# One-hot rows of a gate matrix: one packed bf16 comparison per four tokens, widened by GpSimd and ScalarE

## The chip, the cores and the metric

The kernel runs on one core of a Trainium2 chip. The metric is the device time of one execution in microseconds (us). An execution is profiled once more for the trace; the trace's span runs from the first to the last instruction.

The engines are named as in the profile: PE is TensorE's matrix products (PEld its weight loads), DVE is VectorE, ACT is ScalarE, POOL is GpSimd, SP is SyncE, which issues most of the transfers (DMA). POOL issues the indirect ones.

## What is computed

The reference is one decoder layer over 1024 tokens of width 1024: modulated norm, a mix of retention and stick-breaking attention, and then a feed-forward part of 16384 single-neuron experts. Only that last part is touched here:

```python
def peer(h, w_query, sub_keys, expert_down, expert_up):
    qry = (ht @ w_query).reshape(T, PEER_HEADS, 2, PEER_HALF)
    sub_scores = jnp.einsum('thpc,hpkc->thpk', qry, sub_keys).astype(jnp.float32)
    top_s, top_i = lax.top_k(sub_scores, K)
    ...
    best_s, best_c = lax.top_k(cand_s.reshape(T, PEER_HEADS, K * K), K)
    expert_id = jnp.take_along_axis(cand_id.reshape(T, PEER_HEADS, K * K), best_c, axis=-1)
    gate = jax.nn.softmax(best_s, axis=-1)
    ...
        a = jnp.einsum('pd,ped->pe', xb, u).astype(jnp.float32)
        act = jax.nn.gelu(a, approximate=False) * gb
        return jnp.einsum('pe,ped->pd', act.astype(xb.dtype), v)
```

Each token has 8 heads with 16 chosen experts each, so 128 slots. An expert's number is 128 i1 + i2, where i1 and i2 come from two halves of 128 sub-keys.

## The kernel before

The 1024 tokens are eight tiles of 128. Tiles 0 to 3 are "gathered": for each of their 128 slots the rows of the two expert tables are fetched by an indirect transfer (L767, issued by GpSimd), and VectorE multiplies them with the tokens (L778) or sums them up (L788). That is 1024 gathers in all, through four buffers named g. Tiles 4 to 7 (512 tokens) are "dense": PE computes all 16384 experts for them, in 128 blocks of 128 (`stage1`, L812, and `stage2`, L917), and a gate matrix, zero for the experts that a token has not chosen, multiplies the activations in between (L907).

The instructions are ordered in each engine's queue by a planner that simulates a timeline (`schedule_with_timeline_sim`). The gathers come last in the program and run wherever the rest leaves room; 16 of them, from row 480 on, are held until piece 4 of the gate matrix (`HOLD`, `HOLD_C`).

The gate matrix is built ahead of the dense blocks, at L843 to L876, in 16 pieces of 32 tokens (`CT`), each of eight quads of four tokens. With the 128 slots on partitions, `rt` holds i1, i2 and the gate for each token. For a quad:

- `oa` (128 slots x 4 tokens x 128) is one where i1 equals the column number: a comparison on VectorE (L859). GpSimd multiplies it by the gate (L860).
- `ob` is the same for i2. For three of four quads VectorE compares (L864); for the fourth ScalarE computes max(0, 1 - |i - i2|) in eight instructions (L868, L869).
- PE multiplies them, token by token (L871), which gives 128 x 128 gates of a token, and ScalarE copies the sums out (two copies, at L872 to L874) to `st`, which SP stores (L876).

Between the pieces lie the routing of tiles 5, 6 and 7 (`late`, through `topk`, which ends in `to_slots`) and the first products of early expert blocks (`stage1_ahead`). `stage1` splits the block's weights in two parts for PE: a copy on ScalarE and a subtraction (L810), which `stage1_ahead` gives to GpSimd for n below 8 and for odd n, and otherwise to VectorE. `NSE` is 6 and `NS` is 8; 28 blocks (`NP`) are computed ahead. `oa` and `ob` come from a pool of eleven buffers, `p2`, as do the outputs of some early blocks. `copy` (L70) is ScalarE's activation Copy, so all its instructions stand on L71.

Of the kernel before, what the change touches and what calls it, by code (L numbers as in the profile page):

```python
# [10 lines left out]
F32 = mybir.dt.float32  # L11
F32R = mybir.dt.float32r
BF16 = mybir.dt.bfloat16
I32 = mybir.dt.int32
U32 = mybir.dt.uint32
AF = mybir.ActivationFunctionType
OP = mybir.AluOpType
# [7 lines left out]
SEGS = [(0, 1), (1, 3), (4, 4)]  # L25
NG = 4                      # token tiles whose experts are gathered; the rest see every expert
TD = (NT - NG) * 128
GB = 4                      # expert blocks that share one accumulation
CT = 32                     # tokens of one piece of the gate matrix
NB = 128  # L30
LC = 1, 5, 9                # pieces of the gate matrix ahead of which the next tile is routed
# order of the retention's halves and the stick-breaking projections
RET = "h0 K h1 t0 Q h2 t1 V h3 t2 | t3"
HOLD, HOLD_C = 480, 4      # gathers from row HOLD on wait for piece HOLD_C of the gate matrix
LT0, LATE = 3, (4,)         # gathered tiles from LT0 on are routed ahead of the dense groups from LATE on
# early blocks: PM of a group, NS of them kept on chip, NSE ahead of the gate matrix and NSL behind it
PM, NS, NSE, NSL = 2, 8, 6, 6
NP = 28                     # expert blocks whose first product runs while the gate matrix is built
BIG = 1e15
# [15 lines left out]
def tile_kernel(ctx, tc, A, out):  # L55
# [14 lines left out]
    def copy(out_, in_, scale=1.0):  # L70
        ACT.activation(out_, in_, AF.Copy, scale=scale)  # L71
# [10 lines left out]

    # ------------------------------------------------------------ constants
    ident = cst.tile([128, 128], F32, name="ident")
# [14 lines left out]
    POOL.memset(epsc, EPS)  # L99
    iota128 = cst.tile([128, 128], F32, name="iota128")  # L100
    POOL.iota(iota128, pattern=[[1, 128]], base=0, channel_multiplier=0, allow_small_or_imprecise_dtypes=True)
    iota16 = cst.tile([128, 16], BF16, name="iota16")
# [23 lines left out]

    # ------------------------------------------------------------ modulation and rotary tables
    sc2 = cst.tile([128, 8, 32], F32, name="sc2")
    aw = A["ada_w"].rearrange("(k p) n -> k p n", p=128)

    def mod_pass(c0, nj, W, V):
        # 512 nj columns of silu(c) @ ada_w + ada_b from c0 on, and where they go
        acc = pstile("acc", 4)
        m = 32 * nj
        for kt in range(KT):
            for hf in range(nj // 2):
                w = W(KT * hf + kt)
                SP.dma_start(w, aw[kt, :, c0 + D * hf:c0 + D * hf + D])
                for j2 in range(2):
                    j = 2 * hf + j2  # L140
                    PE.matmul(acc[32 * j:32 * j + 32], sc2[:, kt, :], w[:, 512 * j2:512 * j2 + 512],
                              start=kt == 0, stop=kt == KT - 1, skip_group_check=True)
        brow, modrow = V(), V()
        ab = A["ada_b"]
        for j in range(nj):
            SP.dma_start(brow[32 * j:32 * j + 32], bass.AP(tensor=ab.tensor, offset=ab.offset + c0 + 512 * j,
                                                          ap=[[0, 32], [1, 512]]))
        DVE.tensor_add(modrow[:m], acc[:m], brow[:m])
        tp = pstile("tp", 2)
        for q in range(4):  # L150
            PE.transpose(tp[:, 128 * q:128 * q + m], modrow[:m, 128 * q:128 * q + 128], ident[:m, :m])
        mc = modcol[:, c0 // 128:c0 // 128 + 4 * nj].rearrange("a (j q) -> a j q", q=4)
        DVE.tensor_copy(mc, tp.rearrange("a (q j r) -> a j q r", j=4, r=32)[:, 0:nj, :, 0])
        for j in range(nj):
            v = ("shift1", "scale1", "gate1", "shift2", "scale2", "gate2")[c0 // D + j // 2]
            if v in rows_d:
                SP.dma_start(rows_d[v][:, 512 * (j % 2):512 * (j % 2) + 512], modrow[32 * j:32 * j + 1])
            if v == "scale1" and j % 2:
                DVE.scalar_tensor_tensor(g1s, modcol[:, 8:16], 1.0, n1g, op0=OP.add, op1=OP.mult)
            if v == "scale2" and j % 2:  # L160
                DVE.scalar_tensor_tensor(g2s, modcol[:, 32:40], 1.0, n2g, op0=OP.add, op1=OP.mult)

    with tc.tile_pool(name="ini", bufs=1) as ini:
# [3 lines left out]
        DVE.tensor_copy(sc2, sc[:, :, None].to_broadcast([128, 8, 32]))  # L167
        # sin and cos of position * frequency, reduced exactly in three pieces
        posi = ini.tile([128, NT], I32, name="posi")
# [51 lines left out]

    # ------------------------------------------------------------ gather pools (live through the end)
    gp = ctx.enter_context(tc.tile_pool(name="gp", bufs=1))
# [6 lines left out]
    def seg_gen(phase, t0, nt, hooks):  # L230
        wp, tp_, up, vp, kp = phase
        n = nt * 128
        whole = nt == 1             # one tile alone: float32 products, no split of the weights
        tiles = range(t0, t0 + nt)
# [13 lines left out]
        def stream(src, c0, lhs, evac, transposed):  # L248
            # 512 columns of src from c0 against the operand [128, KT, n]
            acc = [pstile("acc", 4) for _ in range(4 if transposed else nt)]  # L250
# [78 lines left out]

        # ---- norm1 and transposed h  # L330
        xn = []
# [8 lines left out]

        # ---- retention operands
        def rot(acc, o, t):
# [45 lines left out]

        # ---- stick-breaking operands
        def head_norm(acc, o):  # L390
# [28 lines left out]

        # ---- retention  # L420
        def ret_head(i):
# [76 lines left out]

        # ---- stick-breaking attention
        def sb_weights(i, pr):  # L500
# [82 lines left out]

        # ---- output projection, residual
        x1 = []
# [36 lines left out]

        # ---- queries, scores, the 16 best sub-keys of each half
        own = [i for i, t in enumerate(tiles) if t not in sc_d]
# [55 lines left out]
    def topk(kp, v, ix, t, h0, nh):  # L680
# [12 lines left out]
        for h in range(nh):  # L693
# [5 lines left out]
            DVE.max_index(px[:, h, 8:16], bs[:, h, 8:16], c2)  # L699
        # position in the candidate list -> (a, b)  # L700
        pq, qf = K("pq", (2, nh, 16), U32, "w1"), K("qf", (2, nh, 16), F32, "w2")
# [29 lines left out]
        if t < NG:  # L731
            ids = gp.tile([128, nh * 16], I32, name=f"ids_{t}_{h0}")
            DVE.scalar_tensor_tensor(ids, flat(ii[:, 0]), 128.0, flat(ii[:, 1]), op0=OP.mult, op1=OP.add)
        # softmax gates
        e, s = K("ge", (nh, 16)), K("gs", (nh,))
# [14 lines left out]
    def to_slots(t, ii, gt):  # L750
        # routing of this tile with (head, slot) on partitions
        tp = pstile("acc", 4)
        for k, src in enumerate((flat(ii[:, 0]), flat(ii[:, 1]), flat(gt))):
            PE.transpose(tp[:, 128 * k:128 * k + 128], src, ident)
        rt = gp.tile([128, 3, 128], F32, name=f"rt_{t}")
        copy(rt, tp[:, 0:384].rearrange("p (a b) -> p a b", b=128))
        route[t] = rt

# [39 lines left out]
    def dense(Hhi, Hlo, dp, kpg, late):  # L798
# [29 lines left out]
        def stage1_ahead(n):  # L828
            y = stage1(list(pre)[n], POOL if n < NS else (DVE, POOL)[n % 2])
            if n < NS:  # L830
# [11 lines left out]

        # gate matrix, 32 tokens at a time, while the first blocks' products run  # L843
        iota4 = iota128[:, None, :].to_broadcast([128, 4, 128])
        for c in range(TD // CT):
            for k in range(1, 4):
                if c == LC[k - 1]:
                    late[k - 1]()
            rt = route[NG + c * CT // 128]
            st = [U8([128, NB // 2, CT], F32) for _ in range(2)]  # L850
            for q in range(CT // 4):
# [3 lines left out]

                def wide(v):
                    return rt[:, v, t4:t4 + 4, None].to_broadcast([128, 4, 128])

                DVE.tensor_tensor(oa, iota4, wide(0), op=OP.is_equal)  # L859
                r = POOL.tensor_tensor(oa, oa, wide(2), op=OP.mult)  # L860
                if c == HOLD_C:
                    hold = r.ins
                if q % 4:
                    DVE.tensor_tensor(ob, iota4, wide(1), op=OP.is_equal)  # L864
                else:
                    # the same one-hot rows as max(0, 1 - |i - i2|)
                    for k in range(4):
                        ACT.activation(ob[:, k], iota128, AF.Abs, bias=rt[:, 1, t4 + k:t4 + k + 1], scale=-1.0)  # L868
                        ACT.activation(ob[:, k], ob[:, k], AF.Relu, scale=-1.0, bias=1.0)  # L869
                for k in range(4):  # L870
# [17 lines left out]
        for g0 in range(0, NB, GB):  # L888
# [54 lines left out]
            if g0 + GB == NB:  # L943
                # the residual and what is summed up so far, ahead of the last products
                fin = dp2.tile([128, 2, D], F32, name="fin", tag="gm", bufs=2)
# [32 lines left out]

    # the gathers run wherever what is above leaves room
    for t in range(NG):  # L980
# [54 lines left out]
```

## Time and profile before

| | us |
|---|---|
| median of 3 runs | 3257.86 |
| lowest and highest | 3248.1, 3262.58 |
| profiled execution, span | 3254.1 |
| profiled execution, its own device time | not shown by the page |

Where the span goes, by the windows of the trace:

| stretch, us | what it is |
|---|---|
| 0 to 1400 | attention and routing of the first tiles, with gathers among them |
| 1400 to 1527 | routing of tile 4 |
| 1527 to 1886 | gate matrix, early blocks, routing of tiles 5 to 7 |
| 1886 to 3244 | dense blocks, with the rest of the gathers among them |
| 3244 to 3254 | the last sums and stores |

A row of a group of instructions reads: line, engine, operation, output and inputs by the program's names, shapes, count, then busy us and mean ns of one, then the idle time of the engine just before them and what ended most of it. A row of a window gives its length and then, for PE, PEld, DVE, ACT and POOL in turn, the busy time and the number of instructions; then the granted clock of TensorE as a share of full speed, the transfers' share, and GB/s.

### The profile page before, as it was taken

To read this page: it belongs to the slowest core of one execution; us is meant where nothing else is said; L and a number is where in the kernel's file an instruction comes from. 1 tells how busy PE (TensorE), PEld (TensorE's weight loads), DVE (VectorE), ACT (ScalarE), POOL (GpSimd) and SP (SyncE) were. 2 spreads that over 40 slices of the span, in tenths; PEclk is the share of its full clock that TensorE was granted. 3 is DMA by queue.
4 is the path that set the end of the run, shared out by engine and by line. 5 is a ranking of instruction groups with operands and counts; after the bars stand their busy time and mean duration, and the time that the engine had idled before them with its cause. 6 is when DMAs were issued, how large, how long until landed. Compare 5 with 4: busy or idle time off the path is not lost.

```text
span 3254.1 us, 38714 instructions
## 1 busy us (share of the span) xinstructions
PE 2721.3 (84%) x12308; PEld 2102.5 (65%) x12308; DVE 2706.5 (83%) x4997; ACT 1065.1 (33%) x1995; POOL 1956.1 (60%) x1554
## 2 busy tenths in 40 slices
PE   6967867787867678796787799878999999999998
PEld 2454644486654345575666677667787888887786
DVE  2269788799988898799999978999787878777888
ACT  1132223344312344333554532323222322222221
POOL 0026765676677566743577756555666666666664
PEclk9978886898977778897898899998999999999999
DMA  8687876997888666841366789878999999999897
GB/s 317 239 300 271 303 266 218 319 340 258 278 277 281 224 214 226 308 148 65 117 228 211 274 314 329 288 260 297 319 330 328 323 340 339 338 332 319 319 323 273
DMA packets 337644, 899.20 MB, mean 276 GB/s; under 512 B 38296, under 2 KB 105880, under 8 KB 333344
## 3 DMA queue, kind: packets, MB, share of 16 engines
q0 software_dynamic: 147456, 536.94, 47.3%
q1 hardware_dynamic: 189984, 359.80, 32.1%
q8 instruction: 97, 1.59, 0.2%
q14 instruction: 107, 0.88, 0.1%
HBM read 846.24 MB, written 50.35 MB: 276 GB/s over the span
## 4 chain that ended last, share of the span: by engine, by line
DVE 28%; DMA 22%; issue 19%; PE 14%; POOL 14%; ACT 1%; SPq 1%; POOLq 0%; DVEq 0%; ACTq 0%
POOL g L767 9%; DMA g<-in_up_dram,ids 9%; DMA g<-in_down_dram,ids 5%; DVE g L778 5%; DVE gy L788 4%; PE acc L263 2%; DVE p L859 2%; POOL u L810 2%; DMA gm<-gd 2%; DMA rawu<-in_up_dram 1%; POOL wlo L271 1%; DVE p L864 1%; PE acc L871 1%; PE tp L819 1%; PE tp L820 1%
## 5 line engine op out<-in xcount | busy, mean ns | idle before, releaser
L767 POOL DMA_INDIRECT g<-in_up_dram,ids x512 | 583.4, 1139 | 416.3 <-DVE gy L788 295.2
L767 POOL DMA_INDIRECT g<-in_down_dram,ids x512 | 541.6, 1058 | 460.8 <-DVE g L778 280.6
L788 DVE SCALAR_TENSOR_TENSOR gy<-g,a,gy 128x1024 f32<-128x1024 f32 x508 | 651.2, 1282 | 141.2 <-DMA g<-in_up_dram,ids 137.6
L778 DVE SCALAR_TENSOR_TENSOR g<-g,gy 128x1024 f32<-128x1024 f32 x512 | 617.5, 1213 | 133.5 <-DMA g<-in_down_dram,ids 131.3
L928 PE MATMUL acc<-u,p 128*128 128x512 f32 x1024 | 404.6, 400 | 43.5 <-DVE yacc L941 23.9
L819 PE MATMUL tp<-Thi,dhi 128*128 128x512 f32 x1024 | 408.9, 399 | 22.9 <-ACT dhi L71 18.4
L821 PE MATMUL tp<-Thi,dlo 128*128 128x512 f32 x1024 | 405.4, 396 | 3.7 <-POOL dlo L810 3.6
L820 PE MATMUL tp<-Tlo,dhi 128*128 128x512 f32 x1024 | 406.1, 397 | 0.0
L929 PE MATMUL acc<-u,p 128*128 128x512 f32 x1024 | 404.1, 396 | 1.0 <-POOL u L810 1.0
L930 PE MATMUL acc<-u,p 128*128 128x512 f32 x1024 | 386.6, 396 | 15.9 <-DVE p L910 15.9
L810 POOL TENSOR_TENSOR u<-rawu,u 128x1024 fp32r<-128x1024 f32 x128 | 309.0, 2422 | 30.2 <-ACT u L71 28.3
L271 POOL TENSOR_TENSOR wlo<-wraw,whi 128x512 fp32r<-128x512 f32 x182 | 236.6, 1306 | 101.3 <-ACT whi L71 69.1
L928 PEld LDWEIGHTS acc<-u,p 128*128 128x128 f32 x1024 | 195.8, 191 | 99.5 <-DVE yacc L941 32.4
L819 PEld LDWEIGHTS tp<-Thi,dhi 128*128 128x128 f32 x1024 | 196.8, 192 | 65.0 <-ACT dhi L71 19.4
L930 PEld LDWEIGHTS acc<-u,p 128*128 128x128 f32 x1024 | 195.4, 191 | 60.4 <-DVE p L910 19.3
L71 ACT ACTIVATE whi<-wraw 128x512 fp32r<-128x512 f32 x208 | 130.3, 630 | 308.0 <-PE acc L281 100.2
L280 PE MATMUL acc<-wlo,Thi 128*128 128x512 f32 x504 | 214.1, 425 | 18.0 <-POOL wlo L271 17.6
L71 ACT ACTIVATE dhi<-rawd 128x1024 fp32r<-128x1024 f32 x128 | 135.4, 1058 | 284.2 <-PE tp L820 267.2
L71 ACT ACTIVATE u<-rawu 128x1024 fp32r<-128x1024 f32 x128 | 133.2, 1056 | 285.8 <-DMA rawu<-in_up_dram 184.9
L821 PEld LDWEIGHTS tp<-Thi,dlo 128*128 128x128 f32 x1024 | 196.2, 192 | 46.0 <-POOL dlo L810 5.3
L929 PEld LDWEIGHTS acc<-u,p 128*128 128x128 f32 x1024 | 196.0, 191 | 41.2 <-POOL u L810 1.4
L820 PEld LDWEIGHTS tp<-Tlo,dhi 128*128 128x128 f32 x1024 | 196.6, 192 | 39.9
(273 smaller groups left out, 5150.0 us busy)
## 6 DMA issues: line engine op xcount, KB each, us to landing
rawd<-in_downT_dram SPq DMA_DIRECT2D x128, 512.0 KB
rawu<-in_up_dram SPq DMA_DIRECT2D x128, 512.0 KB
gd<-u SPq DMA_DIRECT2D x32, 1024.0 KB
gm<-gd SPq DMA_DIRECT2D x512, 64.0 KB
wraw<-in_w_in_dram SPq DMA_DIRECT2D x112, 256.0 KB
u<-in_ada_w_dram SPq DMA_DIRECT2D x46, 512.0 KB
wraw<-in_wq_dram SPq DMA_DIRECT2D x64, 256.0 KB
u<-in_w_in_dram SPq DMA_DIRECT2D x28, 512.0 KB
```

Of the source, the lines that this page charges most:

```text
L71: ACT.activation(out_, in_, AF.Copy, scale=scale)
L271: (POOL if kt else DVE).tensor_sub(lo, raw, hi.bitcast(F32))
L767: POOL.indirect_dma_start(out=g, out_offset=None, in_=A[src], in_offset=bass.IndirectOffsetOnAxis(ap=groups[j // m][0][:, j % m:j % m + 1] ...
L778: DVE.scalar_tensor_tensor(g, g, 1.0, hp, op0=OP.mult, op1=OP.mult, accum_out=a[:, j:j + 1])
L788: DVE.scalar_tensor_tensor(y, g, a[:, j:j + 1], y, op0=OP.mult, op1=OP.add)
L810: eng.tensor_sub(lo, raw, hi.bitcast(F32))
L819: PE.matmul(a, dhi[:, sl], Hhi[:, kt], start=kt == 0, stop=False)
L820: PE.matmul(a, dhi[:, sl], Hlo[:, kt], start=False, stop=False)
L821: PE.matmul(a, dlo[:, sl], Hhi[:, kt], start=False, stop=kt == KT - 1)
L928: PE.matmul(y, phi[:, sl], uhi[:, ds_], start=st and b == 0, stop=False)
L929: PE.matmul(y, phi[:, sl], ulo[:, ds_], start=False, stop=False)
L930: PE.matmul(y, plo[:, sl], uhi[:, ds_], start=False, stop=sp and b == GB - 1)
```

## The change

Both comparisons of a quad become one VectorE instruction on packed bf16: tile, i1 and i2, column number and token are its axes, `[128, 2, 128, 4]`, with the four tokens innermost. The column numbers are stored four times over in bf16, and the routing of a tile is kept as bf16 numbers (`rb`) and f32 gates (`rg`), by two copies for one. GpSimd's product reads the first half of the result with the axes exchanged, so with a step of four bf16 elements, and writes `oa` in f32. A ScalarE copy does the same for the second half and writes `ob`. The eight ScalarE instructions of every fourth quad are gone. The result `oc` takes a third buffer of `p2` for each quad. The subtraction of the early blocks goes to GpSimd for n below `NSE` and otherwise to VectorE. The rest of the diff is comments.

```diff
-    iota128 = cst.tile([128, 128], F32, name="iota128")
-    POOL.iota(iota128, pattern=[[1, 128]], base=0, channel_multiplier=0, allow_small_or_imprecise_dtypes=True)
+    iota128 = cst.tile([128, 128, 4], BF16, name="iota128")
+    POOL.iota(iota128, pattern=[[1, 128], [0, 4]], base=0, channel_multiplier=0, allow_small_or_imprecise_dtypes=True)
...
     def to_slots(t, ii, gt):
...
-        rt = gp.tile([128, 3, 128], F32, name=f"rt_{t}")
-        copy(rt, tp[:, 0:384].rearrange("p (a b) -> p a b", b=128))
-        route[t] = rt
+        rb = gp.tile([128, 2, 128], BF16, name=f"rb_{t}")
+        copy(rb, tp[:, 0:256].rearrange("p (a b) -> p a b", b=128))
+        rg = gp.tile([128, 128], F32, name=f"rg_{t}")
+        copy(rg, tp[:, 256:384])
+        route[t] = rb, rg
...
-            y = stage1(list(pre)[n], POOL if n < NS else (DVE, POOL)[n % 2])
+            y = stage1(list(pre)[n], POOL if n < NSE else DVE)
...
-        iota4 = iota128[:, None, :].to_broadcast([128, 4, 128])
+        iota8 = iota128[:, None, :, :].to_broadcast([128, 2, 128, 4])
...
-            rt = route[NG + c * CT // 128]
+            rb, rg = route[NG + c * CT // 128]
...
-                def wide(v):
-                    return rt[:, v, t4:t4 + 4, None].to_broadcast([128, 4, 128])
-
-                DVE.tensor_tensor(oa, iota4, wide(0), op=OP.is_equal)
-                r = POOL.tensor_tensor(oa, oa, wide(2), op=OP.mult)
+                oc = P2([128, 2, 128, 4], BF16)
+                DVE.tensor_tensor(oc, iota8, rb[:, :, None, t4:t4 + 4].to_broadcast([128, 2, 128, 4]), op=OP.is_equal)
+                r = POOL.tensor_tensor(oa, oc[:, 0].rearrange("p i t -> p t i"),
+                                       rg[:, t4:t4 + 4, None].to_broadcast([128, 4, 128]), op=OP.mult)
...
-                if q % 4:
-                    DVE.tensor_tensor(ob, iota4, wide(1), op=OP.is_equal)
-                else:
...
-                    for k in range(4):
-                        ACT.activation(ob[:, k], iota128, AF.Abs, bias=rt[:, 1, t4 + k:t4 + k + 1], scale=-1.0)
-                        ACT.activation(ob[:, k], ob[:, k], AF.Relu, scale=-1.0, bias=1.0)
+                copy(ob, oc[:, 1].rearrange("p i t -> p t i"))
```

## Rows read from the trace of the kernel before

**Rows 1.** The page's totals by engine: busy us, share, instructions.

```profile
PE 2721.3 (84%) x12308; PEld 2102.5 (65%) x12308; DVE 2706.5 (83%) x4997; ACT 1065.1 (33%) x1995; POOL 1956.1 (60%) x1554
```

**Rows 2.** Windows: busy us of each engine, granted clock, DMA share, GB/s.

```profile
1527.00:1886.00 359.00, 277.33 (x1549) 240.89 (x1548) 349.31 (x485) 195.46 (x575) 260.28 (x183) 0.88 0.57 203
1886.00:3244.00 1358.00, 1292.25 (x5561) 1052.09 (x5559) 1137.14 (x1629) 378.22 (x490) 848.39 (x632) 0.98 0.90 317
...
2000.00:2300.00 300.00, 258.73 (x1055) 205.04 (x1055) 279.38 (x608) 85.61 (x109) 177.89 (x130) 0.93 0.85 289
2300.00:2600.00 300.00, 293.42 (x1280) 240.49 (x1279) 247.49 (x245) 82.79 (x107) 192.56 (x143) 0.99 0.92 328
2600.00:2900.00 300.00, 298.74 (x1316) 246.45 (x1315) 240.74 (x369) 87.46 (x112) 198.10 (x152) 1.00 0.95 337
```

**Rows 3.** Groups by line, VectorE, 1527 to 1886 us.

```profile
L859 DVE TENSOR_TENSOR p<-iota,rt 128x512 f32<-128x512 f32 x128 | 146.6, 1154 | 0.0
L864 DVE TENSOR_TENSOR p<-iota,rt 128x512 f32<-128x512 f32 x96 | 88.6, 923 | 7.2 <-PE acc L871 7.2
...
L810 DVE TENSOR_TENSOR dlo<-rawd,dhi 128x1024 fp32r<-128x1024 f32 x9 | 13.8, 1529 | 0.0
...
L726 DVE TENSOR_TENSOR oh<-oh,iota 128x2048 bf16<-128x2048 bf16 x6 | 9.4, 1574 | 2.0 <-ACT oh L71 2.0
```

**Rows 4.** Groups by line, GpSimd, 1527 to 1886 us.

```profile
L860 POOL TENSOR_TENSOR p<-p,rt 128x512 f32<-128x512 f32 x128 | 165.6, 1304 | 79.4 <-DVE p L859 78.4 <-PE acc L871 0.5
...
L810 POOL TENSOR_TENSOR dlo<-rawd,dhi 128x1024 fp32r<-128x1024 f32 x12 | 32.4, 2703 | 0.8 <-ACT dhi L71 0.7
```

**Rows 5.** Timeline, VectorE and GpSimd, 1706.5 to 1712: start us, us.

```profile
1708.10 2.95 DVE L711 TENSOR_TENSOR qf<-qf,m 128x128 f32<-128x128 f32 x1
1710.97 0.28 DVE L710 TENSOR_TENSOR ab<-ab,m 128x128 f32<-128x128 f32 x1
...
1707.86 3.03 POOL L860 TENSOR_TENSOR p<-p,rt 128x512 f32<-128x512 f32 x3
```

**Rows 6.** Single lines, whole run: duration ns min/median/max, first and last start.

```profile
L859 DVE TENSOR_TENSOR p<-iota,rt x128: 637/680/4717, 1527.3 to 1878.2; 128x512 f32<-128x512 f32 x128
...
L726 DVE TENSOR_TENSOR oh<-oh,iota x34: 398/426/3356, 197.1 to 2252.2; 128x512 bf16<-128x512 bf16 x24, 128x2048 bf16<-128x2048 bf16 x10
...
L860 POOL TENSOR_TENSOR p<-p,rt x128: 1028/1058/8106, 1528.0 to 1880.2; 128x512 f32<-128x512 f32 x128
...
L810 POOL TENSOR_TENSOR dlo<-rawd,dhi x18: 2342/2406/3356, 1507.3 to 1897.9; 128x1024 fp32r<-128x1024 f32 x18
```

**Rows 7.** Groups by line, ScalarE, whole run.

```profile
L71 ACT ACTIVATE whi<-wraw 128x512 fp32r<-128x512 f32 x208 | 130.3, 630 | 308.0 <-PE acc L281 100.2 <-DMA wraw<-in_w_in_dram 92.7 <-DMA wraw<-in_wq_dram 47.4
...
L868 ACT ACTIVATE p<-iota,rt 128x128 f32<-128x128 f32 x128 | 40.9, 412 | 0.0
...
L869 ACT ACTIVATE p<-p 128x128 f32<-128x128 f32 x128 | 31.5, 323 | 0.0
```

**Rows 8.** Waits, 1527 to 1886: us in total, times, longest.

```profile
POOL p L860 <- DVE p L859: 78.4, 68, 7.1
```

**Rows 9.** Windows of L767 alone: GpSimd busy us (gathers issued).

```profile
1527.00:1886.00 359.00, 61.84 (x42) 0.88 0.57 203
...
2300.00:2900.00 600.00, 250.23 (x236) 1.00 0.93 332
```

**Rows 10.** Timeline of the end.

```profile
3242.88 0.39 PE L930 MATMUL acc<-u,p 128*128 128x512 f32 x1
...
3250.16 0.33 SPq L796 DMA_DIRECT2D out_dram<-g  x1
```

## The prediction

> **What bounds the kernel now.** I read the page's totals first [rows 1]: VectorE (DVE) and TensorE (PE) are both busy about 83% of the span, so no engine is the bound everywhere and the total decides nothing. The windows by stage [rows 2] separate two regimes. From 1527 to 1886 us, the stretch in which the one-hot rows of L859 and L864 are made, DVE is busy 349.3 of 359 us while PE shows 277.3, GpSimd (POOL) 260.3 and ScalarE (ACT) 195.5. From 1886 us on, in the dense expert products, PE takes over: 293.4 of 300 us and 298.7 of 300 us in the two windows from 2300 to 2900, with the transfers at a share of 0.92 and 0.95; only 2000 to 2300, where one more tile is routed, is again DVE's (279.4 of 300). So this change acts on a stage where DVE is the bound, and what it gains must then pass through a stage that runs at the pace of PE and of the transfers.
>
> The groups by line inside the stage [rows 3] show what fills DVE there: 128 comparisons at L859 (146.6 us) and 96 at L864 (88.6 us), together 235.2 us, two thirds of its time. Their means, 1154 and 923 ns, are far above the median of 680 ns of the same instruction [rows 6]. The difference is no arithmetic. In the timeline [rows 5] a DVE subtraction of 128x128 begins at 1708.10 and takes 2.95 us, while its neighbour of the same shape takes 0.28; it ends within 0.2 us of the end of three GpSimd products that ran from 1707.86 to 1710.89. A DVE instruction with two operands in SBUF and a GpSimd instruction stand in each other's way, and the time is booked as busy on whichever came second. GpSimd pays too: its product has a median of 1058 ns [rows 6] and a mean of 1304 [rows 4]. So in this stage DVE's 349.3 us are real work plus about 128 x 0.474 + 96 x 0.243 = 84 us of standing behind GpSimd. The waits [rows 8] say the rest: GpSimd waits 78.4 us for L859, so it is led, not leading.
>
> **The change, part by part.** (1) Comparisons. L859 and L864 go: -235.2 us of DVE. In their place come 128 instructions that compare 1024 packed bf16 elements each. No such shape is in the trace, but the routing's is_equal on packed bf16 is [rows 3, 6]: L726 takes 398 ns at its least for 512 elements. The f32 comparison of 512 elements takes 637 ns at its least, so the packed form does two elements in the time of one, and 1024 packed elements should cost what 512 f32 ones do: 0.68 us. The bounds: 0.68, and, if the four-element runs of the token operand stop the packing, 1024 elements one by one, 0.68 + 512 x (637 - 398) / 256 ns = about 1.16 us. I take 0.68, because L726 already has a repeated operand and is packed. To it belongs a share of standing behind GpSimd: I keep the 0.47 us of L859, though there is less GpSimd work to stand behind, because the comparison keeps two SBUF operands. That gives 128 x 1.154 = +147.7 us; with no standing at all it would be 87.
>
> (2) Splits. The weight split of the early blocks goes to DVE for n = 6, 7 and for odd n from 9 to 27, 12 instructions in all. DVE takes 1.53 us each inside this stage [rows 3]: +18.3 us. GpSimd loses 12 at a median of 2.41 us [rows 6]: -29 us. The transfers, the ACT copy and the order of SP's queue stay; only the subtraction changes engine. Behind it on DVE stand comparisons and the products of gathered rows, which the sum covers since DVE is counted as the bound.
>
> (3) GpSimd's product reads one operand as bf16 with a step of four elements. No GpSimd instruction in the trace reads so. The nearest row is today's product, same shape, same repeated operand, 1.06 us alone and 1.30 in the stage; I keep it. From below, nothing suggests a gain. From above I take twice the mean, 2.6 us, for the rival below.
>
> The Trainium skill ("GPSIMD Engine Reference", section 7) states that GpSimd reads slow by about half when step times element size passes 8 bytes; here it is exactly 8, so by that rule the product stays as it is. No row here shows it. Were it past the limit, 0.53 us x 128 = 68 us would come onto GpSimd, an estimate from that page, and it would stand level with the 300 us that I expect of the stage.
>
> (4) ACT drops 128 Abs and 128 Relu instructions, 40.9 + 31.5 = 72.4 us, and gets 128 copies of 128x512, at the 630 ns of the weight copy with that shape [rows 7] 80.6 us: ACT goes from 195 to about 204 us, well covered by 359 or 300. What is new is that every quad now passes ACT, in order with the evacuations; today three of four don't. That copy lies beside GpSimd's product, which takes twice as long, so it costs nothing unless ACT is over a microsecond behind.
>
> (5) Small things. Each routed tile gets two ACT copies for one, some 0.3 to 0.4 us more by the 128x128 rows [rows 7], four times: 1.5 us at most, hidden by ACT's idle time. The wider iota is made by GpSimd at the start, over a thousand us before its first reader. Each quad takes three of the eleven p2 buffers where it took two, so 3.7 quads are in flight instead of 5.5. At 2.3 us per quad (300 / 128) that is 8.6 us of life for a chain of about 1.2 + 1.3 + 1 us: enough. If that cover fails, the comparison waits for PE's read, as L864 does today for 7.2 us in all [rows 3], and the products of gathered rows wait behind it on DVE.
>
> Sum for DVE in the stage: 349.3 - 235.2 + 147.7 + 18.3 = 280 us. GpSimd: 260 - 29 = 231. PE stays at its 277.3, at a mean granted clock of 0.88 [rows 2]. DVE and PE then stand level at 280, and two engines that feed each other through GpSimd and ACT don't both run without gaps. I add 20 us and expect the stage at 300 us: -59. Its bounds are 280 (-79) and, for unpacked comparisons, 349.3 - 235.2 + 128 x (1.16 + 0.47) + 18.3 = 341 (-18).
>
> Passing on to the end: the dense products start 59 us sooner and PE's last one, now at 3242.9 [rows 10], moves by that much if nothing else changes. But the gathered tiles end last, at 3250.2 [rows 10], and they share the stage: 42 gathers are issued in it [rows 9]. At the same rate, 300 us hold 35, and 7 go into the dense stage, where 236 take 600 us [rows 9], 2.54 us each: +18. The end moves by 59 - 18 = 41 us. Span 3254.1 - 41 = 3213. The page gives no device time of its own for this execution; the median of the runs, 3257.86, lies 3.8 us above the span, and I carry this over: **3217 us**.
>
> **The rivals.** *Gathers eat it.* The order of the queues is planned by a simulated timeline, and gathers run where it sees room. If a shorter, denser stage holds only 20 of the 42, the other 22 at 2.54 us take 56 us of the 59 back: about 3255. For it speaks the transfer share of 0.95 late in the dense stage; against it that the stage itself has a share of 0.57 [rows 2], so there is room for them, and DVE is what is being freed. *The comparison isn't packed.* Stage 341 us, less the gathers pushed out, 2 x 2.54: about 3245. *GpSimd becomes the bound*, on the slower side. With 61.8 us of gather issues [rows 9], the stage is longer than today once a product with its waiting passes (359 - 62) / 128 = 2.32 us; at 2.6 us it is 395 us, +36, and 3294. For it speaks only that no row shows a strided bf16 read there. *More comes through*: the planner puts the gathers into DVE's freed time, stage 280 and nothing given back: -79, 3179.
>
> **Chances.** Forecast (3195 to 3238) 0.48; more comes through 0.18; gathers eat it 0.13; unpacked 0.09; GpSimd bound or a worse planned order in the dense stage 0.12. Half a percent, 16 us, is about what a measurement of this kernel can tell from no change: the runs before spread over 14.5 us. Faster takes the first two and a sliver of unpacked: 0.67; same takes most of the gathers' and the unpacked case: 0.19; slower 0.14. The range leaves out the GpSimd case and the far end of the good one: 3172 to 3258.
>
> **What would show it.** Packed: the new comparison at about 0.68 us median. Standing: its mean at 1.0 to 1.2 us. GpSimd's product: median near 1.06. The stage, first to last comparison: 300 us instead of the 351 between the first and the last L859 [rows 6], with PE's granted clock no lower. Gathers issued in it: 35. Wrong would make me a GpSimd median above 1.7 us (with today's 0.25 of standing, 128 x 1.95 + 62 = 312 us, past the stage I expect), a PE that waits for the ACT copy, or a dense stage longer than its 1358 us by more than the 18 us.

## The result, and the profile after

The changed kernel takes 3201.82 us (median; 3194.32 to 3221.45), the kernel before 3260.22 in the runs beside it: a ratio of 0.9848, with a 95% interval of 0.9821 to 0.9876. The forecast of 3217 us was a ratio of 0.9875 to the median then known, at the upper edge of that interval. The profiled execution took 3201.63 us, 1.8 more than its span.

The page's totals, as in [rows 1], hardly differ:

```profile
PE 2693.4 (84%) x12308; PEld 2079.8 (65%) x12308; DVE 2631.3 (82%) x4913; ACT 1076.0 (34%) x1871; POOL 1918.6 (60%) x1542
```

The windows by stage do, beside the first two of [rows 2]; the first comparison starts at 1523.6 us, and the stage ends with the last product of the gate matrix:

```profile
1523.00:1828.00 305.00, 255.68 (x1527) 220.63 (x1526) 275.49 (x404) 203.52 (x445) 218.21 (x176) 0.94 0.67 242
1828.00:3185.00 1357.00, 1291.80 (x5574) 1053.06 (x5573) 1135.21 (x1625) 380.51 (x494) 841.63 (x626) 0.98 0.90 316
```

Read to the same point, the last such product at 1885 us, the stage of the kernel before lasts 358 us ([rows 2] runs 1 us further). Now it lasts 305. From there to PE's last product, the dense stage takes 1356 us against 1358. The stage starts 4 us sooner, and from PE's last product to the end it now takes 16 us where it took 11: -4 - 53 - 2 + 5 = -54 us, the difference of the spans. So nearly the whole gain is made in the stage that was changed, and none of it is given back in the dense one. VectorE is busy 275.5 of the 305 us. PE's busy time fell too, from 277.3 to 255.7, with 22 of 1549 products fewer in the window: the mean granted clock in the stage rose from 0.88 to 0.94 of the full 2.4 GHz level. The same shows inside the stage: 56 products of the gate matrix keep PE busy for 7.2 us from 1740 to 1760 us, at a clock of 1.00, and for 8.7 us from 1660 to 1680, at 0.84.

Groups by line inside the stage, on VectorE, GpSimd and ScalarE in turn, which answer to [rows 3, 4]:

```profile
L860 DVE TENSOR_TENSOR p<-iota,rb 128x1024 bf16<-128x1024 bf16 x128 | 138.0, 1099 | 16.9 <-POOL p L861 7.4 <-PE acc L867 7.2 <-ACT p L71 1.3
...
L812 DVE TENSOR_TENSOR dlo<-rawd,dhi 128x1024 fp32r<-128x1024 f32 x19 | 31.4, 1655 | 2.2 <-ACT dhi L71 2.2
...
L861 POOL TENSOR_TENSOR p<-p,rg 128x512 f32<-128x512 bf16 x128 | 154.5, 1218 | 70.7 <-DVE p L860 55.4 <-DVE gs L739 5.4 <-PE acc L867 2.9
...
L812 POOL TENSOR_TENSOR dlo<-rawd,dhi 128x1024 fp32r<-128x1024 f32 x2 | 5.3, 2634 | 1.2 <-ACT dhi L71 1.2
...
L71 ACT ACTIVATE p<-p 128x512 f32<-128x512 bf16 x128 | 87.2, 686 | 70.4 <-DVE p L860 67.8 <-POOL p L861 2.2
```

Single lines over the whole run, least, median and most, as [rows 6]:

```profile
L860 DVE TENSOR_TENSOR p<-iota,rb x128: 670/728/3464, 1523.6 to 1820.5; 128x1024 bf16<-128x1024 bf16 x128
...
L861 POOL TENSOR_TENSOR p<-p,rg x128: 1033/1060/2037, 1524.5 to 1822.1; 128x512 f32<-128x512 bf16 x128
```

The comparison of 1024 packed elements takes 0.73 us in the median and 0.67 at its least; its mean is 1099 ns, so it still stands behind GpSimd for about 0.4 us a time (0.37 above the median, 0.43 above the least). GpSimd's product with a bf16 operand at a step of four has the median of the one before it, 1.06 us. ScalarE's widening copy takes 686 ns.

Waits inside the stage (us in total, times, longest), beside [rows 8]:

```profile
ACT p L71 <- DVE p L860: 67.8, 55, 3.7
POOL p L861 <- DVE p L860: 55.4, 44, 7.2
...
DVE p L860 <- POOL p L861: 7.4, 8, 1.4
DVE p L860 <- PE acc L867: 7.2, 6, 2.8
```

VectorE now waits for others, which it hardly did: the comparison waits for a p2 buffer until GpSimd or PE has read it. Gathers issued in the stage and in the dense stage, as [rows 9]:

```profile
1523.00:1828.00 305.00, 56.15 (x45) 0.94 0.67 242
1828.00:3185.00 1357.00, 537.57 (x499) 0.98 0.90 316
```

45 gathers lie in the shorter stage, three more than in the longer one before. In both kernels 480 gathers come ahead of the first comparison, and those of the stage start only when piece 4 has released them, at 1651.7 us before and at 1629.5 now. So 42 were issued in 233 us before, and 45 in 199 us now. The timeline of the end, as [rows 10]:

```profile
3183.69 0.39 PE L926 MATMUL acc<-u,p 128*128 128x512 f32 x1
...
3195.79 0.33 SPq L798 DMA_DIRECT2D out_dram<-g  x1
```

PE's last product comes 59 us sooner than before, the last store 54.

### The profile page after: what moved, and what is told of

It reads as the page before. It is cut to its first block, busy times and chain, and to the rows that moved or that the text cites. A ratio compares the mean times of both kernels' runs of the same rounds, so it can differ in the third digit from the quotient of the medians.

```text
span 3199.8 us, 38483 instructions
## 1 busy us (share of the span) xinstructions
PE 2693.4 (84%) x12308; PEld 2079.8 (65%) x12308; DVE 2631.3 (82%) x4913; ACT 1076.0 (34%) x1871; POOL 1918.6 (60%) x1542
## 4 chain that ended last, share of the span: by engine, by line
DVE 27%; PE 21%; DMA 21%; issue 15%; POOL 12%; ACT 2%; SPq 1%; POOLq 0%; DVEq 0%; ACTq 0%
DMA g<-in_up_dram,ids 10%; POOL g L769 8%; DVE g L780 5%; DMA g<-in_down_dram,ids 4%; DVE gy L790 4%; PE tp L821 2%; PE tp L822 2%; PE tp L823 2%; PE acc L263 2%; DMA rawu<-in_up_dram 2%; DVE p L860 2%; PE acc L924 2%; PE acc L926 2%; PE acc L925 2%; DVE dlo L812 1%
## 5 line engine op out<-in xcount | busy, mean ns | idle before, releaser
L769 POOL DMA_INDIRECT g<-in_up_dram,ids x512 | 594.8, 1162 | 404.7 <-DVE gy L790 281.2
L780 DVE SCALAR_TENSOR_TENSOR g<-g,gy 128x1024 f32<-128x1024 f32 x512 | 617.9, 1213 | 134.1 <-DMA g<-in_down_dram,ids 132.2
L280 PE MATMUL acc<-wlo,Thi 128*128 128x512 f32 x504 | 212.5, 422 | 16.1 <-POOL wlo L271 15.6
```

What stands on the lines that cost most here:

```text
L769: POOL.indirect_dma_start(out=g, out_offset=None, in_=A[src], in_offset=bass.IndirectOffsetOnAxis(ap=groups[j // m][0][:, j % m:j % m + 1] ...
L780: DVE.scalar_tensor_tensor(g, g, 1.0, hp, op0=OP.mult, op1=OP.mult, accum_out=a[:, j:j + 1])
```

## The experiments

Two theories were tried against each other first. **A**: the gain is VectorE's time, since the packed comparison does twice as many elements in the time of one, and the rest of its cost is standing behind GpSimd. **B**: the gain is the relief of GpSimd by the twelve splits. All ratios are to the kernel before, in the same batch of runs.

**The splits put back** (e1).

```diff
-            y = stage1(list(pre)[n], POOL if n < NSE else DVE)
+            y = stage1(list(pre)[n], POOL if n < NS else (DVE, POOL)[n % 2])
```

> The changed kernel with the weight splits of the early blocks given to GpSimd and VectorE as before (12 splits go back to GpSimd). Theory A, the packed comparison is the gain: VectorE loses 12 x 1.65 = 20 us of splits in the stage but stands 12 more times behind a GpSimd instruction of 2.4 us, so the time stays within 15 us of the changed kernel's 3202: 3187 to 3217, and the stage between 290 and 315 us. Rival B, the relief of GpSimd by the moved splits is the gain: the stage goes back towards 340 us and the time to 3230 or more.

Measured: 3204.72 us, 0.9851 (0.9824 to 0.9878), the ratio of the changed kernel. VectorE's groups in its stage of 313 us:

```profile
L860 DVE TENSOR_TENSOR p<-iota,rb 128x1024 bf16<-128x1024 bf16 x128 | 155.7, 1239 | 16.8 <-POOL p L861 7.8 <-PE acc L867 7.7 <-ACT p L71 1.2
...
L812 DVE TENSOR_TENSOR dlo<-rawd,dhi 128x1024 fp32r<-128x1024 f32 x9 | 13.8, 1529 | 3.7 <-PE acc L867 3.7
```

Against the changed kernel, VectorE does 17.6 us less of splits (13.8 instead of 31.4) and 17.7 us more of comparisons (155.7 instead of 138.0) with the same 128 comparisons. What it hands to GpSimd it gets back as standing. On top of the packed comparison the splits are worth nothing measurable; B is out as the cause of the gain.

**The splits moved in the kernel before** (e2).

```diff
-            y = stage1(list(pre)[n], POOL if n < NS else (DVE, POOL)[n % 2])
+            y = stage1(list(pre)[n], POOL if n < NSE else DVE)
```

> The kernel before with only the splits moved (GpSimd for n below 6, VectorE otherwise). Theory A: within 15 us of before's 3260, so 3245 to 3275, since VectorE, the bound of the stage, gets 20 us more work and stands less. Rival B: most of the gain, 3205 to 3230, and a stage below 325 us.

Measured: 3240.08 us, 0.9955 (0.9937 to 0.9973): a gain of about 15 us, more than A allowed for in that kernel and far from what B needs.

```profile
L859 DVE TENSOR_TENSOR p<-iota,rt 128x512 f32<-128x512 f32 x128 | 141.6, 1114 | 0.0
L864 DVE TENSOR_TENSOR p<-iota,rt 128x512 f32<-128x512 f32 x96 | 81.0, 844 | 0.0
...
L810 DVE TENSOR_TENSOR dlo<-rawd,dhi 128x1024 fp32r<-128x1024 f32 x19 | 29.1, 1534 | 0.0
```

Ten more splits on VectorE cost 15 us (13.8 to 29.1), and 224 comparisons stand 13 us less (235.2 to 222.6). The books are nearly even here as well, and VectorE is busy for 347 us of the stage, as it was for 348, yet the stage is 348 us instead of 358 by the same measure. These 9 us are VectorE's idle time, which falls from 10 us to 1: the 7.2 us for which L864 waited for PE [rows 3] are gone. Why they went is not shown; the queues are ordered anew in every kernel.

**An operand that isn't packed** (e3).

```diff
-    iota128 = cst.tile([128, 128, 4], BF16, name="iota128")
+    iota128 = cst.tile([128, 128, 4], F32, name="iota128")
```

> The changed kernel with the column numbers in f32, so that one operand of the comparison isn't 16 bits wide; nothing else differs. Theory A, the gain is that two elements go through at once: the comparison's median rises from 0.73 to about 1.2 us, 128 x 0.48 = 61 us come onto VectorE, 30 us of which its idle time in the stage may take: stage 335 to 365 us, time 3230 to 3262. Rival C, the gain is that there are 128 instructions instead of 224, each with its own standing behind GpSimd: stage under 320 us and time 3200 to 3215.

Measured: 3255.7 us, 0.9996 (0.997 to 1.0022): the whole gain is gone. The comparison over the whole run, the groups of VectorE in its stage, and the gathers issued there:

```profile
L860 DVE TENSOR_TENSOR p<-iota,rb x128: 1167/1633/3377, 1518.2 to 1896.7; 128x1024 bf16<-128x1024 f32 x128
```

```profile
L860 DVE TENSOR_TENSOR p<-iota,rb 128x1024 bf16<-128x1024 f32 x128 | 209.4, 1644 | 1.1 <-POOL p L861 0.9 <-PE acc L867 0.2
L780 DVE SCALAR_TENSOR_TENSOR g<-g,gy 128x1024 f32<-128x1024 f32 x35 | 41.9, 1208 | 4.9 <-DMA g<-in_down_dram,ids 4.8
```

```profile
1518.00:1911.00 393.00, 113.92 (x71) 0.83 0.63 226
```

At its least the comparison takes 1.17 us, the 1.16 that the prediction had worked out for this case. The stage grew by 88 us to 393, more than expected. The comparisons take 209.4 us instead of 138.0, and wait 16 us less (1.1 instead of 16.9). The stage also holds 71 gathers instead of 45; 26 times VectorE's 1.28 us (the product at L780, 1.21, and the reading of its sum) is 33 us: 71 - 16 + 33 = 88 us, which is all of it. The gathers run until the stage ends, so a longer stage takes in more of them, and each makes it longer; the two can't be told apart here. That the number of instructions alone brings the gain, rival C, is out: there are 128 of them here too.

**GpSimd's product twice in every second quad** (e5).

```diff
-                r = POOL.tensor_tensor(oa, oc[:, 0].rearrange("p i t -> p t i"),
+                for _ in range(1 + q % 2):
+                    r = POOL.tensor_tensor(oa, oc[:, 0].rearrange("p i t -> p t i"),
```

> The changed kernel with GpSimd's product made twice in every second quad (the same result written again), 64 x 1.06 = 68 us more on GpSimd in the stage, where it is busy 218 of 305 us and so has 87 us idle. Theory A, VectorE's comparison with two SBUF operands and a GpSimd instruction stand in each other's way: the comparison's mean rises from 1.10 us to 1.3 or more though its own work is the same, the stage grows by 25 to 45 us, time 3225 to 3250. Rival E, GpSimd's idle time takes the second product: the mean stays at 1.0 to 1.15 us, the stage under 312 us, time 3195 to 3210.

Measured: 3274.24 us, 1.0075 (1.0051 to 1.0099).

```profile
L860 DVE TENSOR_TENSOR p<-iota,rb 128x1024 bf16<-128x1024 bf16 x128 | 152.3, 1203 | 19.2 <-POOL p L862 12.6 <-PE acc L868 4.2 <-issue 2.3
```

```profile
1529.00:1930.00 401.00, 98.48 (x83) 0.85 0.65 236
```

The mean rose to 1203 ns, less than the 1.3 us of the expectation, while the stage grew by 96 us to 401, more than it said. It holds 83 gathers, 38 more than in the changed kernel, and 38 x 1.28 = 49 us of VectorE's time are theirs. Some 47 us remain for the 68 us of second products, so that GpSimd's idle time takes them (E) is out. Of these, A's standing is only the smaller part: the comparisons take 14 us more (152.3 against 138.0). PE waits 85 us for GpSimd's product where it waited 33, so GpSimd being late for PE counts here as well, and the gathers blur the size of both.

**No product at all, in the kernel before** (e7).

```diff
-                DVE.tensor_tensor(oa, iota4, wide(0), op=OP.is_equal)
-                r = POOL.tensor_tensor(oa, oa, wide(2), op=OP.mult)
+                r = DVE.tensor_tensor(oa, iota4, wide(0), op=OP.is_equal)
```

> The kernel before without GpSimd's product: PE gets the bare one-hot rows, the gates are left out. Theory A, the 84 us that the comparisons take beyond their 0.68 us is standing behind that product: the means of the two comparisons fall from 1154 and 923 ns to below 780, VectorE in the stage from 349 to about 270 us, the stage to 275 to 300 us, time 3185 to 3215. Rival F, they stand behind the gathers' issues and the splits, or the time is their own: the means stay above 900 ns, the stage above 335 us, time 3240 to 3260.

Measured: 3358.57 us, 1.0332 (1.0275 to 1.0388), which neither theory had. The time says nothing about either: the release of the gathers now names a VectorE comparison, and it no longer held them. From 1400 to 1700 us, where the kernel before issues 13 gathers, this one issued

```profile
1400.00:1700.00 300.00, 123.80 (x130) 0.70 0.81 276
```

130 of them, 119 ahead of the first comparison, which at VectorE's 1.28 us each are some 150 us; it came only at 1666.5 us, 139 later than in the kernel before. The means can still be read:

```profile
L859 DVE TENSOR_TENSOR p<-iota,rt 128x512 f32<-128x512 f32 x128 | 88.7, 706 | 0.0
...
L863 DVE TENSOR_TENSOR p<-iota,rt 128x512 f32<-128x512 f32 x96 | 70.2, 731 | 1.2 <-PE acc L870 1.2
...
L810 DVE TENSOR_TENSOR dlo<-rawd,dhi 128x1024 fp32r<-128x1024 f32 x9 | 10.9, 1216 | 0.0
```

706 and 731 ns instead of 1154 and 923, for the same instructions, and 1216 instead of 1529 for VectorE's splits.

**The product over 16 of 128 columns, in the kernel before** (e12), which keeps the release where it was.

```diff
-                r = POOL.tensor_tensor(oa, oa, wide(2), op=OP.mult)
+                r = POOL.tensor_tensor(oa[:, :, 0:16], oa[:, :, 0:16], wide(2)[:, :, 0:16], op=OP.mult)
```

> The kernel before with GpSimd's product over 16 of its 128 columns, so that the gathers are held by the same instruction as before; the gates of the other 112 columns are left out. Theory A, the comparisons stand behind the product: their means fall below 850 ns, VectorE has 60 us or more less to do, the stage is 285 to 310 us and the time 3190 to 3220, unless the planner fills the room with gathers; then the stage is longer by 1.3 us for each beyond 42. Rival F: means above 900 ns, stage above 335 us, 3240 to 3260.

Measured: 3197.24 us, 0.9824 (0.9788 to 0.986).

```profile
L859 DVE TENSOR_TENSOR p<-iota,rt 128x512 f32<-128x512 f32 x128 | 97.9, 777 | 4.8 <-PE acc L871 3.5 <-POOL p L860 1.3
L864 DVE TENSOR_TENSOR p<-iota,rt 128x512 f32<-128x512 f32 x96 | 75.2, 783 | 0.2 <-PE acc L871 0.2
```

```profile
1524.00:1811.00 287.00, 242.63 (x1522) 215.10 (x1521) 275.14 (x482) 188.35 (x569) 170.02 (x183) 0.93 0.69 250
```

Without touching a comparison, the stage falls to 287 us and the comparisons from 235.2 to 173.1 us. F is out: what they took beyond 0.68 us was mostly standing behind the product. The stage of the kernel before could be shortened from either side, by less VectorE work or by less GpSimd work.

**The gathers held until piece 12** (e4).

```diff
-HOLD, HOLD_C = 480, 4
+HOLD, HOLD_C = 480, 12
```

> The changed kernel with the gathers from row 480 on held until piece 12 of the gate matrix instead of piece 4, which takes some 25 to 30 of the 45 gathers out of the stage. Theory A of the prediction, a gather pushed into the dense stage costs 2.54 us at the end: the last gather ends 60 to 75 us later than the shortened stage would let it, net 3225 to 3270, PE's last product comes before the last gather by 30 us or more. Rival D, the dense stage has room for more gathers and PE sets the end: the stage gets 20 to 35 us shorter for VectorE and the time falls to 3165 to 3190.

Measured: 3241.65 us, 0.9951 (0.9933 to 0.9969). Gathers in the stage, and the end:

```profile
1550.00:1839.00 289.00, 23.25 (x19) 0.96 0.54 202
```

```profile
3184.80 0.39 PE L926 MATMUL acc<-u,p 128*128 128x512 f32 x1
...
3251.43 0.34 SPq L798 DMA_DIRECT2D out_dram<-g  x1
```

26 gathers fewer lie in the stage, which is 15 us shorter, and PE's dense products take 10 us less (1346 against 1356). But from PE's last product to the end of the span (3255.4) there are now 70.6 us instead of 16.1: 54.5 / 26 = 2.1 us for each gather. Part of that is PE being done sooner: from the end of the stage to the end of the span it is 1416 us instead of 1372, 44 / 26 = 1.7 us for each. The profiled execution is the slowest of the ten, at 3257.09 us, and its stage starts 26 us later than that of the changed kernel, which no gather in the stage explains; by the ratios the loss against the changed kernel is about 34 us (0.9951 against 0.9848). Both theories named a true part, and the gathers decide the end.

**One comparison per eight tokens** (e8).

```diff
-                oc = P2([128, 2, 128, 4], BF16)
-                DVE.tensor_tensor(oc, iota8, rb[:, :, None, t4:t4 + 4].to_broadcast([128, 2, 128, 4]), op=OP.is_equal)
+                if q % 2 == 0:
+                    oc = dp.tile([128, 4, 128, 4], BF16, name="oc", bufs=2)
+                    DVE.tensor_tensor(oc, iota8, rb[:, t4 // 4:t4 // 4 + 2].rearrange("p g v t -> p (g v) t")[:, :, None, :]
+                                      .to_broadcast([128, 4, 128, 4]), op=OP.is_equal)
...
-            return dp.tile(shape, dt, name="p2", tag="p2", bufs=11)
+            return dp.tile(shape, dt, name="p2", tag="p2", bufs=8)
```

> The changed kernel with one comparison per eight tokens: 64 of 2048 packed elements, at 1.21 us by the routing's comparison of that size, in a buffer of its own (two of 4 KB, for which p2 goes from 11 to 8 buffers, in the dense stage too). Theory G, each comparison stands about once however long it is: 64 x (1.21 + 0.4) = 103 us instead of 138, stage 270 to 290 us, time 3170 to 3192. Theory A in the form that standing follows GpSimd's time and not the number of comparisons: 77 + 50 = 127 us, stage 290 to 305 us, time 3190 to 3205. Rival H, the fewer p2 buffers cost more in the dense stage: its length passes 1375 us and the time 3215.

Measured: 3292.92 us, 1.0123 (1.0073 to 1.0174).

```profile
L860 DVE TENSOR_TENSOR oc<-iota,rb 128x2048 bf16<-128x2048 bf16 x64 | 108.9, 1708 | 26.6 <-POOL p L862 19.0 <-ACT p L71 4.1 <-ACT u L71 3.2
```

```profile
1530.00:1817.00 287.00, 246.88 (x1504) 218.39 (x1503) 249.34 (x328) 195.64 (x441) 226.26 (x168) 0.95 0.66 240
1817.00:3287.00 1470.00, 1324.89 (x5595) 1073.64 (x5594) 1153.17 (x1643) 382.31 (x500) 845.81 (x635) 0.95 0.85 297
```

The stage is 287 us, as G said (its 64 comparisons take 108.9 us, 103 by G), but the dense stage takes 1470 us: rival H, and far beyond the 20 us that it named.

**The same with a pool of its own for `oc`, and p2 at eleven** (e10).

```diff
+        ocg = tc.tile_pool(name="ocp", bufs=1, side="right")
+        ocp = ocg.__enter__()
...
-                    oc = dp.tile([128, 4, 128, 4], BF16, name="oc", bufs=2)
+                    oc = ocp.tile([128, 4, 128, 4], BF16, name="oc", bufs=2)
...
-            return dp.tile(shape, dt, name="p2", tag="p2", bufs=8)
+            return dp.tile(shape, dt, name="p2", tag="p2", bufs=11)
```

> One comparison per eight tokens again, but its two 4 KB buffers come from a pool that is closed ahead of the dense stage, and p2 keeps its eleven buffers. If the eight buffers of p2 were what lengthened the dense stage to 1475 us: stage 275 to 295 us as there, dense stage back at 1345 to 1365 us, time 3175 to 3195. If the new order of the queues was it, the dense stage stays above 1400 us and the time above 3240.

Measured: 3216.68 us, 0.9867 (0.9837 to 0.9898).

```profile
L862 DVE TENSOR_TENSOR oc<-iota,rb 128x2048 bf16<-128x2048 bf16 x64 | 110.2, 1732 | 16.2 <-POOL p L864 15.5 <-ACT p L71 0.8
```

```profile
1536.00:1828.00 292.00, 56.24 (x37) 0.95 0.62 227
```

```profile
1536.00:1828.00 292.00, 247.51 (x1490) 212.91 (x1489) 259.86 (x325) 194.76 (x442) 228.49 (x167) 0.95 0.62 227
1828.00:3193.00 1365.00, 1303.92 (x5610) 1062.22 (x5608) 1125.45 (x1630) 383.53 (x497) 849.60 (x630) 0.98 0.90 317
```

With eleven buffers the dense stage is back at 1365 us, so the eight buffers were its cost. The stage stays at 292 us, yet the kernel is no faster than the changed one, and slower than the 3175 to 3195 us expected: only 37 gathers lie in the stage, and the last one is issued 12 us after PE's last product. In this profile the stage also starts 12 us later than in the changed kernel.

**The same, released at piece 2** (e11).

```diff
-HOLD, HOLD_C = 480, 4
+HOLD, HOLD_C = 480, 2
```

> The same with the gathers from row 480 on released at piece 2 instead of 4. The changed kernel's last gather ends 12 us after PE's last product, and a shorter stage leaves more of such a tail. If gathers set the end there: some 8 more gathers in the stage, 1.3 us of VectorE each, the tail gone, 5 to 15 us under the run with piece 4. If PE sets it: the stage grows by 10 us and so does the time.

Measured: 3202.66 us, 0.9843 (0.981 to 0.9875): 14 us under e10 in the median, but the two intervals overlap, and level with the changed kernel. As expected if gathers set the end, 46 lie in the stage instead of 37, and the time from PE's last product to the end falls from 28 us to 10. But the dense stage takes 11 us more, and the two profiles' stages start 20 us apart, so what the release alone is worth is not shown. The comparisons stand longer here:

```profile
L862 DVE TENSOR_TENSOR oc<-iota,rb 128x2048 bf16<-128x2048 bf16 x64 | 123.5, 1933 | 18.2 <-POOL p L864 17.5 <-ACT p L71 0.8
```

at 1933 ns against 1732 in e10, for the same 2048 elements. That is nearer to the 127 us of e8's theory A than to the 103 of G, so whether standing goes by the number of comparisons or by GpSimd's time stays open.

**A step of eight elements** (e9).

```diff
-                oc = P2([128, 2, 128, 4], BF16)
+                oc = P2([128, 128, 2, 4], BF16)
...
-                copy(ob, oc[:, 1].rearrange("p i t -> p t i"))
+                copy(ob, oc[:, :, 1].rearrange("p i t -> p t i"))
```

> The changed kernel with the two comparisons' results interleaved, so that GpSimd's product and ScalarE's copy read their bf16 operand with a step of eight elements instead of four; sizes and counts stay. If the step doesn't matter: product 1.06 us median, time 3195 to 3210. If it does: 1.5 us or more, 60 us more on GpSimd, a comparison that stands longer, stage 325 us or more and time 3220 to 3250. The Trainium skill (GPSIMD Engine Reference, section 7) states that reads of step times size over 8 bytes cost about half more; 16 bytes are over it.

Measured: 3231.62 us, 0.9939 (0.9914 to 0.9965), stage 337 us. The product over the whole run, and ScalarE's copy in the stage:

```profile
L861 POOL TENSOR_TENSOR p<-p,rg x128: 1261/1309/2358, 1520.0 to 1851.7; 128x512 f32<-128x512 bf16 x128
```

```profile
L71 ACT ACTIVATE p<-p 128x512 f32<-128x512 bf16 x128 | 149.4, 1171 | 46.7 <-DVE p L860 44.1 <-POOL p L861 1.7 <-ACT u L71 0.2
```

Both readers slow down: GpSimd's product from 1.06 to 1.31 us, less than the 1.5 us of the expectation, and ScalarE's copy from 686 to 1171 ns. So the loss can't be put down to GpSimd alone.

**Every fourth product on ScalarE** (e13).

```diff
+                if q % 4 == 0:
+                    for k in range(4):
+                        ACT.activation(oa[:, k], oc[:, 0, :, k], AF.Copy, scale=rg[:, t4 + k:t4 + k + 1])
+                else:
...
```

> The changed kernel with the gate product of every fourth quad on ScalarE, four copies of 128x128 scaled by the token's gate, instead of on GpSimd. ScalarE is busy 203 of 305 us in the stage and gets 32 x 4 x 0.41 = 53 us more; GpSimd loses 32 x 1.06 = 34 us, and with it the comparisons lose a share of their 51 us of standing, some 13. If ScalarE's room covers the copies: comparison's mean below 1.05 us, stage 285 to 298 us, time 3183 to 3198. If the copies make ScalarE late for PE, since evacuations stand behind them: stage 305 us or more, PE waiting for ScalarE by 20 us or more, time 3202 to 3225.

Measured: 3188.95 us, 0.9775 (0.9748 to 0.9802), clear of the changed kernel's interval: the best version here.

```profile
L860 DVE TENSOR_TENSOR p<-iota,rb 128x1024 bf16<-128x1024 bf16 x128 | 123.6, 985 | 16.7 <-ACT p L71 6.1 <-DMA ad<-p 4.7 <-PE acc L871 3.2
...
L863 ACT ACTIVATE p<-p,rg 128x128 f32<-128x128 bf16 x128 | 42.3, 411 | 21.8 <-DVE p L860 19.1 <-POOL p L865 2.7
```

```profile
1531.00:1822.00 291.00, 249.20 (x1502) 216.50 (x1501) 254.99 (x405) 234.13 (x568) 173.54 (x144) 0.95 0.68 252
1822.00:3182.00 1360.00, 1300.57 (x5595) 1062.47 (x5593) 1141.37 (x1624) 383.70 (x501) 847.99 (x626) 0.98 0.90 317
```

The comparison's mean falls to 985 ns with the same work, ScalarE takes its 42 us, and the stage is 291 us, as the expectation had it.

## Why the prediction was right, point by point

**The comparison** was sized well: 138.0 us in the stage against 147.7 forecast, with a little more time of its own (0.73 us against 0.68) and a little less standing. Its own time is that of the packed case, and e3 shows that the packing carries the gain: without it, the ratio is 0.9996.

**The standing behind GpSimd** was the right mechanism, and e12 shows it from GpSimd's side. The Trainium skill ("GPSIMD Engine Reference", section 8) lists contention of GpSimd with VectorE instructions of two SBUF inputs; the runs agree, with means of 1154 and 923 ns that fall to 777 and 783 when the product shrinks.

**The splits** were mis-sized. The prediction booked +18.3 us on VectorE and kept the 0.47 us of standing, although it had named the smaller GpSimd work. Both moved: ten more splits in the stage (two of the twelve lie outside it) cost 17.6 us, and the comparisons stood 17.7 us less (e1). The term for the pair is about zero on top of the packed comparison.

**GpSimd's product** at 1.06 us, **ScalarE** at 204 us (203.5 measured) and VectorE's sum of 280 us (275.5 measured) came out. The stage is 305 us where 300 was forecast (from the first comparison to the last, the count in the prediction's signs, 297), but not for the reason given: PE did not stay at 277 us of busy time, and the gap is VectorE waiting for 30 us, for p2 buffers among other things (7.4 + 7.2 us at the comparison), the wait that the prediction had called covered. That the 20 us added for two engines level came near these 30 is luck. The wait for ScalarE's copy, one of its signs of being wrong, cost PE 1.2 us.

**The gathers** were the step that failed. The prediction let their number fall with the stage's length, from 42 to 35, and gave 18 us back. It is piece 4 that starts them, not the stage, and behind it they ran faster, one in 4.4 us instead of 5.6. So 45 lie in the shorter stage, and the dense stage kept its length. That VectorE, busy for 90% of the stage instead of 97%, had more room for them fits this, but no run tests it. The price of a gather that is pushed out was of the right order (2.54 us forecast, 1.7 to 2.1 in e4); the number was wrong. With the 18 us left out, the sum would have been 3254.1 - 59 + 3.8 = 3199 us against 3202 measured. That it comes so near is partly luck: the stage gave 53 us and not 59, the end 5 us less, while an earlier start gave 4 us, the dense stage 2, and the runs lie 1.8 us above the span and not 3.8.

**The rivals.** *Gathers eat it* named 20 gathers in the stage and 3255 us; e4, with 19, takes 3242, so the mechanism is real, but the changed kernel doesn't meet its condition. *More comes through* was right in half: nothing was given back, but the stage did not reach 280 us. *Unpacked* is the case of e3: 3256 us against 3245, and a stage of 393 us against 341. Its comparisons took 209 us, as it had worked out (128 x 1.63), but the stage held more gathers and not fewer, and VectorE was idle for 25 us of it. That GpSimd becomes the bound needed a product of 2.3 us with its waiting and is out at 1.22; e9 shows that a step twice as long would have brought part of it. The Trainium skill's rule on this ("GPSIMD Engine Reference", section 7) held in its direction on both sides of its 8 bytes, with 1.06 us at 8 and 1.31 at 16; its size did not, with 24% more for the whole instruction and not half.

## What to carry to other kernels

Where VectorE and GpSimd both work on operands in SBUF, take a mean far above the least duration as a sign of standing, and test it by shrinking the other engine's work. The median can hide it: in e1 it is 1210 ns and the least 670. Where the test confirms it, count the two engines' work as partly one queue: moving an instruction between them can be worth nothing (e1), and shrinking either side's work shortens the stage (the change itself and e12); moving some of it to a third engine with room did so too (e13). When low-priority work is placed by a planner, its number in a stage need not follow the stage's length; find what releases it, then fix the number or read it, but don't scale it. And a buffer taken from a shared pool is paid wherever that pool is used: three of eleven cost the dense stage some 105 us (e8, e10).

## What the runs showed that was not expected

- ScalarE's copy of 128x512 bf16 took 686 ns with a step of four elements (8 bytes) and 1171 ns with a step of eight (e9).
- The number of gathers in the stage ranged from 19 to 83 over these kernels (103 in e7). Where it was changed alone, by the release (e4), it cost about 34 us; in e7, where 119 more gathers ran ahead of the stage, the kernel lost more than the whole change brought.
- In the profiles, e7 aside, the stage starts between 1516.5 us (e11) and 1549.8 us (e4), though the work described ahead of it is the same, 480 gathers included. Why is not shown. A profile is one execution, so differences of this size between two spans say nothing about the change.
